# q scaled by its norm over the head's slope where it is made; attention's bias and row maximum by one fused add-scale-minimum per head

## The chip, the core and the metric

The kernel runs on one core of a Trainium2 chip. A core has five engines with one in-order instruction stream each: PE (matmuls; its weight loads are listed as PEld), DVE (the vector engine), ACT (the scalar engine), POOL (GpSimd) and SP, which here only issues DMAs. The metric is device time in microseconds (us), lower is better: the median of three runs was 2928.23 us before the change.

## The reference

A decoder trunk of two layers over 2048 tokens of width 1024: a gated MLP layer, then one layer of dilated sliding-window attention whose keys and values come from a shared projection. Only the attention layer is touched:

```python
q = rms_norm(q, q_norm_g) * (HEAD_DIM ** -0.5)           # per head of 128
# for each of three groups of 8 heads (dilation d = 1, 4, 16), in blocks of 128 queries
sc = jnp.einsum('brnikgh,brnjkh->brnkgij', ql, kb)        # 128 queries x 256 keys (own and previous block)
bias = -slopes * (d * dq)                                 # dq = 128 + i - j
sc = jnp.where(valid, sc + bias, -jnp.inf)
m = jnp.max(sc, axis=-1, keepdims=True)
p = jnp.exp(sc - m)
l = jnp.sum(p, axis=-1, keepdims=True)
o = einsum(p / l, vb);  lse = m + jnp.log(l)
# the groups are then mixed by softmax(lse), gated, and projected out
```

There are 24 query heads, in three groups of 8 with two K/V heads each. Blocks without a previous block see 128 keys, the others 256. `slopes` of head h is 2^(-8(h+1)/24).

## The kernel before

The sequence is cut into four quarters (Q = 0 to 3) of four token tiles of 128. For each quarter the kernel runs the gated MLP layer (`layer_A`: the products v, u, z and o), then the projections of the attention layer (`proj_B`: the K/V blocks `kv_block`, three `q_block`s and a `z_block`). All products are in split precision: each weight tile is loaded by SP (L259, L315), copied to a rounded high part by ACT (L251) and its low part is made by DVE (L252), and PE multiplies three times.

Attention runs as side work ("fillers") between those matmuls. Groups 0 and 1 (`attend_local`) of quarter Q run during `layer_A` of quarter Q+1, and for the last quarter at the very end, between the matmuls of the output projection (`finish`). Group 2 reaches over the whole sequence (`wide_attention`), so it can only start when the last quarter's q of group 2 is stored; it is paced through the last quarter's `kv_block(0)`, `q_block(1)` and `q_block(0)`. One attention unit is a group, a block of 128 queries and one K/V head, with four query heads: 3 x 16 x 2 = 96 units, 42 of them with 128 keys and 54 with 256. Its stages are `att_1` (load of `qt`, transposes `pk` and `pq` on PE, copies to `kT` and `qT`), `att_2` (scores `ps` on PE, bias, maximum, exponentials), `att_3` (transposes `pp` of the probabilities, copy to `pT`), `att_4` (product `po` with the values, copy or sum to `ot`, store).

The code's order isn't the final one: a scheduler with its own cost model sets the order within each engine's stream when the kernel is built, and each stream then runs in that order. The order between engines is kept by semaphores only.

The places that matter here:

- `q_block` (L1215 to L1233). A tile of q of 128 tokens and four heads (512 columns) arrives as `src`. ACT squares it (L1223), DVE sums per head (L1225), and POOL makes four numbers per token with four small instructions (L1226 to L1229): with v the mean square plus epsilon, v^-0.5 goes to columns 516 to 519 of `src` and slope x v^0.5 to columns 512 to 515. q itself stays unscaled. SP stores all 520 columns to `qd` in DRAM (L1232). That store is issued late, five products after; but for group 2 of the last quarter it is only held back by one product (the list `stores` starts at 4 there).
- `att_1` (L1322 to L1351): SP loads `qt` of 520 columns (L1319, two buffers). DVE copies its last 8 columns to `rt` (L1339). PE transposes the four heads (L1343), ACT and DVE make `qT`.
- `att_2` (L1353 to L1404): per head DVE forms `dist` x (slope x v^0.5) + score (L1383, an instruction with one PSUM input; `dist` holds minus the distance, and -1e30 outside the window). It then takes the maximum of the two or four heads that share a PSUM tile (L1386), and makes minus the maximum times v^-0.5 (L1387). For group 0 the result is joined with that of group 1 by a minimum (L1390). ACT takes the exponential per head with v^-0.5 as its scale and L1387's result as its bias (L1393), and sums the row in the same instruction.
- PSUM tiles of attention (`pk`, `pq`, `ps`, `pp`, `po`) share four buffers in the pool `ps`.

Of the kernel before, what the change touches and what calls it, by code (L numbers as in the profile page):

```python
# [12 lines left out]
F32 = mybir.dt.float32  # L13
# [5 lines left out]
P = 128  # L19
D = 1024  # L20
S = 2048
# [13 lines left out]
def trunk(ctx, tc, out, x, c, a_ada_w, a_ada_b, a_norm_g, a_w_in, a_sgu_g, a_w_spatial,  # L35
# [25 lines left out]
    qd = [dp.tile([S, 2, 520], F32, name=f"qd{g}") for g in range(3)]  # L61
# [97 lines left out]
    slopes = cp.tile([P, NH], F32, name="slopes")  # L159
    for h in range(NH):  # L160
        nc.gpsimd.memset(slopes[:, h:h + 1], 2.0 ** (-8.0 * (h + 1) / NH) * DIL[h // 8])
# [380 lines left out]
    def sum_tile(nm):  # L542
        return tp.tile([P, 520], F32, tag="st", name=f"st_{nm}")
# [633 lines left out]
    def proj_B(Q, hk, hb, keep, rest, ahead, ready):  # L1177
# [37 lines left out]
        def q_block(g):  # L1215
            def ev(t, src, n):
                if t < 2 and n == 0:
# [9 lines left out]
                nc.gpsimd.tensor_tensor(src[:, 516:520], s4[:, 4:8], mhalf[:, 0:4], ALU.pow)  # L1227
                nc.gpsimd.tensor_tensor(s4[:, 4:8], s4[:, 4:8], src[:, 516:520], ALU.mult)
                nc.gpsimd.tensor_tensor(src[:, 512:516], s4[:, 4:8],  # L1229
                                        slopes[:, g * 8 + n * 4:g * 8 + n * 4 + 4], ALU.mult)  # L1230
# [86 lines left out]
    def att_q(g, b, kh):  # L1317
        qt = ap_.tile([P, 520], F32, tag="qt", name=f"qt{g}_{b}_{kh}")
        nc.sync.dma_start(qt, blk_rows(qd[g], g, b)[:, kh, :])  # L1319
        return qt  # L1320

    def att_1(u):  # L1322
# [15 lines left out]
        rt = sp.tile([P, 16], F32, tag="rt", name=f"rt{g}_{b}_{kh}")  # L1338
        nc.vector.tensor_copy(rt[:, 0:8], u["qt"][:, 512:520])  # L1339
        u["rt"] = rt  # L1340
# [12 lines left out]
    def att_2(u):  # L1353
# [5 lines left out]
        for c in range(nk):  # L1359
# [21 lines left out]
            for i in range(hp):  # L1381
                h = c * hp + i
                nc.vector.scalar_tensor_tensor(pr[:, i, :], dist[:, 256 - w:256], u["rt"][:, h:h + 1],  # L1383
                                               psc[:, i, :], ALU.mult, ALU.add)
            mx = u["rt"][:, 8 + c * hp:8 + (c + 1) * hp]
            nc.vector.tensor_reduce(mx, pr, AX.X, ALU.max)  # L1386
            nc.vector.scalar_tensor_tensor(mneg, mx, -1.0, u["rt"][:, 4 + c * hp:4 + (c + 1) * hp],  # L1387
                                           ALU.mult, ALU.mult)
            if g == 0:
                nc.vector.tensor_tensor(mneg, mneg, stat[1][:, b, c0:c0 + hp], ALU.min)  # L1390
            for i in range(hp):
                h = 4 + c * hp + i
                nc.scalar.activation(pr[:, i, :], pr[:, i, :], AF.Exp, bias=mneg[:, i:i + 1],  # L1393
                                     scale=u["rt"][:, h:h + 1], accum_out=lsum[:, i:i + 1])
# [318 lines left out]
```

## Time and profile before

| | |
|---|---|
| device time, three runs | 2926.15, 2928.23, 2930.01 us |
| profiled execution, first to last instruction (its span) | 2930.7 us; no other time of that execution is given |
| granted PE clock, mean | 0.998 |
| ACT busy | 1639.0 us, 56% of the span |
| DMA moved | 713.54 MB, mean 243 GB/s |
| `qd` stores and `qt` loads | 96 each of 260 KB; median landing of a `qt` load 3.6 us |

The profile comes from one execution. A group of instructions is named by its line, engine, operation and tiles (output <- inputs), with its count, busy time, mean length in ns, then the engine's idle time just before them and what ended it. In a timeline a row has a start, a length, the engine, the instruction, and in brackets how long its engine had been idle and who ended that. Lengths on an engine overlap: the next instruction often starts before the listed end of the one before, so the distance of two starts is what an instruction really costs its engine. A wait is put down to whatever released it last.

### The profile page before, as it was taken

The page shows a single profiled execution, that of the slowest core. Times are in us where ns is not written, and L with a number is a line of the kernel's source. Part 1 is how long each engine was busy: PE and PEld are TensorE (multiplying, and loading weights), DVE is VectorE, ACT ScalarE, POOL GpSimd, SP SyncE. Part 2 cuts the span into 40 slices and gives each one's busy share as a digit, 9 for nine tenths or more (in the row PEclk, how much of TensorE's full clock was granted, in tenths as well). Part 3 has the DMA queues.
Part 4 walks back from the last instruction along what each step waited for, and adds up shares of the span by engine and source line. Part 5 has one row for each costly group of instructions (what it writes and reads, how often), then busy time and mean ns, then how long its engine had stood idle before and what let it go on. Part 6 is the DMA issues. An engine that isn't in the chain of part 4 may idle for free.

```text
span 2930.7 us, 45684 instructions
## 1 busy us (share of the span) xinstructions
PE 2890.4 (99%) x14642; PEld 2422.7 (83%) x14642; DVE 2166.7 (74%) x4038; ACT 1639.0 (56%) x3378; POOL 758.4 (26%) x1043
## 2 busy tenths in 40 slices
PE   8999999999999999999999999999999999999999
PEld 5788888888888878888888888888888888888887
DVE  6878666787777886877677776877769776888682
ACT  4323355767676365676555365674646366876441
POOL 1057522330000513501223213501414221122312
PEclk9999999999999999999999999999999999999999
DMA  8899976796889976887435976875337967789653
GB/s 285 272 311 336 308 244 184 257 306 203 282 294 315 334 241 210 265 289 249 158 120 202 344 226 203 296 262 162 105 109 260 322 202 224 256 271 332 216 172 112
DMA packets 393813, 713.54 MB, mean 243 GB/s; under 512 B 41723, under 2 KB 141277, under 8 KB 393573
## 3 DMA queue, kind: packets, MB, share of 16 engines
q1 hardware_dynamic: 393572, 710.63, 72.6%
q8 instruction: 116, 1.90, 0.3%
q14 instruction: 125, 1.02, 0.1%
HBM read 552.53 MB, written 157.95 MB: 242 GB/s over the span
## 4 chain that ended last, share of the span: by engine, by line
PE 40%; DMA 3%; issue 3%; DVE 3%; POOL 1%; ACT 1%; SPq 0%; POOLq 0%; ACTq 0%; DVEq 0%
PE po L1453 3%; PE pd_kv L280 3%; PE pd_z L324 2%; PE pd_z L322 2%; PE pd_z L323 2%; PE pd_o3a L280 1%; PE pd_u L322 1%; PE pd_u L324 1%; PE pd_u L323 1%; PE pd_o2a L280 1%; PE pd_v3b L280 1%; PE pf L1637 1%; PE pf L1638 1%; PE pf L1639 1%; DMA qt<-qd 1%
## 5 line engine op out<-in xcount | busy, mean ns | idle before, releaser
L280 PE MATMUL pd_kv<-w_kv,hkh 128*128 128x512 f32 x672 | 209.5, 393 | 1.4 <-DVE w_kv L252 1.3
L322 PE MATMUL pd_u<-hAh,w_u 128*128 128x512 f32 x512 | 207.5, 405 | 0.0
L322 PE MATMUL pd_z<-hAh,w_z 128*128 128x512 f32 x512 | 204.1, 399 | 0.0
L324 PE MATMUL pd_u<-hAh,w_u 128*128 128x512 f32 x512 | 201.0, 393 | 2.3 <-DVE w_u L252 2.3
L323 PE MATMUL pd_u<-hAl,w_u 128*128 128x512 f32 x512 | 200.2, 391 | 0.0
L324 PE MATMUL pd_z<-hAh,w_z 128*128 128x512 f32 x512 | 200.2, 391 | 0.0
L323 PE MATMUL pd_z<-hAl,w_z 128*128 128x512 f32 x512 | 199.5, 390 | 0.0
L1453 PEld LDWEIGHTS po<-kv,pT 128*128 128x128 f32 x1200 | 147.9, 192 | 13.0 <-ACT pT L1299 3.7
L251 ACT ACTIVATE w_u<-raw_u 128x512 fp32r<-128x512 f32 x128 | 79.2, 630 | 135.4 <-DMA raw_u<-in_a_w_in_dram 56.7
L1453 PE MATMUL po<-kv,pT 128*128 128x128 f32 x1200 | 151.2, 276 | 3.6 <-ACT pT L1299 2.5
L251 ACT ACTIVATE w_z<-raw_z 128x512 fp32r<-128x512 f32 x128 | 79.6, 628 | 133.9 <-PE pd_z L324 60.6
L280 PEld LDWEIGHTS pd_kv<-w_kv,hkh 128*128 128x128 f32 x672 | 125.9, 189 | 28.6 <-DVE w_kv L252 2.6
L1401 POOL TENSOR_TENSOR dg<-pr,ident 128x256 f32<-128x256 f32 x38 | 30.9, 813 | 437.2 <-DVE stat L1448 226.6
L252 DVE TENSOR_TENSOR w_z<-raw_z,w_z 128x512 fp32r<-128x512 f32 x128 | 109.4, 868 | 44.9 <-ACT w_z L251 44.6
L280 PE MATMUL pd_kv<-w_kv,hkl 128*128 128x512 f32 x336 | 131.2, 391 | 0.0
L1393 ACT ACTIVATE pr<-pr,stat,rt 128x256 f32<-128x256 f32 (+1 forms) x192 | 104.2, 544 | 33.2 <-DVE stat L1387 20.0
L1226 POOL TENSOR_SCALAR s_q<-s_q 128x4 f32<-128x4 f32 x96 | 26.6, 277 | 351.3 <-DVE s_q L1225 238.8
L252 DVE TENSOR_TENSOR w_u<-raw_u,w_u 128x512 fp32r<-128x512 f32 x128 | 94.1, 745 | 30.8 <-ACT w_u L251 30.0
L324 PEld LDWEIGHTS pd_u<-hAh,w_u 128*128 128x128 f32 x512 | 96.4, 188 | 24.2 <-DVE w_u L252 3.1
L251 ACT ACTIVATE w_q<-raw_q 128x512 fp32r<-128x512 f32 x144 | 88.8, 627 | 48.3 <-PE pd_kv L280 11.2
L252 DVE TENSOR_TENSOR w_q<-raw_q,w_q 128x512 fp32r<-128x512 f32 x144 | 95.8, 687 | 24.9 <-ACT w_q L251 22.9
L324 PEld LDWEIGHTS pd_z<-hAh,w_z 128*128 128x128 f32 x512 | 96.1, 188 | 20.7
(904 smaller groups left out, 8553.1 us busy)
## 6 DMA issues: line engine op xcount, KB each, us to landing
raw_q<-in_b_w_in_dram SPq DMA_DIRECT2D x144, 256.0 KB, 3.4
w_o<-wtd SPq DMA_DIRECT2D x72, 512.0 KB, 5.2
raw_u<-in_a_w_in_dram SPq DMA_DIRECT2D x128, 256.0 KB, 4.2
raw_z<-in_a_w_in_dram SPq DMA_DIRECT2D x128, 256.0 KB, 3.6
wtd<-cs SPq DMA_DIRECT2D x56, 512.0 KB, 4.1
qt<-qd SPq DMA_DIRECT2D x96, 260.0 KB, 3.6
raw_v<-in_a_w_in_dram SPq DMA_DIRECT2D x96, 256.0 KB, 4.1
od<-ot SPq DMA_DIRECT2D x96, 256.0 KB, 3.0
```

Source lines behind the costliest of these rows:

```text
L251: nc.scalar.activation(hi, src, AF.Copy)
L252: nc.vector.tensor_tensor(lo, src, hi.bitcast(F32), ALU.subtract)
L280: last_mm[0] = nc.tensor.matmul(pt, a, u[:, w, :], start=f, stop=e, skip_group_check=more)
L322: nc.tensor.matmul(pts[i], wh, hh[:, k, :], start=k == 0, stop=False)
L323: nc.tensor.matmul(pts[i], wh, hl[:, k, :], start=False, stop=False)
L324: nc.tensor.matmul(pts[i], wl, hh[:, k, :], start=False, stop=k == KT - 1)
L1393: nc.scalar.activation(pr[:, i, :], pr[:, i, :], AF.Exp, bias=mneg[:, i:i + 1], scale=u["rt"][:, h:h + 1], accum_out=lsum[:, i:i + 1])
L1401: nc.gpsimd.tensor_tensor(dg, prev, ident.unsqueeze(1).broadcast_to([P, hp, P]), ALU.mult)
L1453: nc.tensor.matmul(po[:, h * P:(h + 1) * P], u["pT"][h // hp][:, h % hp, j, :], u["kv"][:, j, kh, 1, :], start=j == 0, stop=j == nk - 1)
L1637: nc.tensor.matmul(pt, yb[:, 0, k, :], w_[:, 0, :], start=k == 0, stop=False)
L1638: nc.tensor.matmul(pt, yb[:, 0, k, :], w_[:, 1, :], start=False, stop=False)
L1639: nc.tensor.matmul(pt, yb[:, 1, k, :], w_[:, 0, :], start=False, stop=k == KT - 1)
```

## The change

- q is scaled where it is made: POOL computes v^-0.5, multiplies it by 1 / slope of the head (`steep`), and multiplies all 512 columns of `src` by it, per head, in place. The tiles `src`, `qt` and `qd` lose their 8 extra columns.
- In attention, the copy to `rt`, the bias, the maximum, its scaling and the minimum with group 1 go. In their place stands one `tensor_tensor_reduce` per head: (score + `dist`) x (-slope) is written to `pr`, and its running minimum, which starts from a large number (group 0: from group 1's value), goes to the head's column of `stat`. Because q was divided by the slope, -slope brings minus the biased score.
- ACT's exponential has the constant -1 as its scale.

```diff
-    qd = [dp.tile([S, 2, 520], F32, name=f"qd{g}") for g in range(3)]
+    qd = [dp.tile([S, 2, 512], F32, name=f"qd{g}") for g in range(3)]
...
-    slopes = cp.tile([P, NH], F32, name="slopes")
+    slope = [2.0 ** (-8.0 * (h + 1) / NH) * DIL[h // 8] for h in range(NH)]
+    steep = cp.tile([P, NH], F32, name="steep")
     for h in range(NH):
-        nc.gpsimd.memset(slopes[:, h:h + 1], 2.0 ** (-8.0 * (h + 1) / NH) * DIL[h // 8])
+        nc.gpsimd.memset(steep[:, h:h + 1], 1.0 / slope[h])
...
                 nc.gpsimd.tensor_scalar(s4[:, 4:8], s4[:, 0:4], 1.0 / P, EPS, ALU.mult, ALU.add)
-                nc.gpsimd.tensor_tensor(src[:, 516:520], s4[:, 4:8], mhalf[:, 0:4], ALU.pow)
-                nc.gpsimd.tensor_tensor(s4[:, 4:8], s4[:, 4:8], src[:, 516:520], ALU.mult)
-                nc.gpsimd.tensor_tensor(src[:, 512:516], s4[:, 4:8],
-                                        slopes[:, g * 8 + n * 4:g * 8 + n * 4 + 4], ALU.mult)
+                nc.gpsimd.tensor_tensor(s4[:, 4:8], s4[:, 4:8], mhalf[:, 0:4], ALU.pow)
+                nc.gpsimd.tensor_tensor(s4[:, 4:8], s4[:, 4:8],
+                                        steep[:, g * 8 + n * 4:g * 8 + n * 4 + 4], ALU.mult)
+                heads = src.rearrange("p (h d) -> p h d", d=P)
+                nc.gpsimd.tensor_tensor(heads, heads, s4[:, 4:8].unsqueeze(2).broadcast_to([P, 4, P]),
+                                        ALU.mult)
...
-        rt = sp.tile([P, 16], F32, tag="rt", name=f"rt{g}_{b}_{kh}")
-        nc.vector.tensor_copy(rt[:, 0:8], u["qt"][:, 512:520])
-        u["rt"] = rt
...
             for i in range(hp):
-                h = c * hp + i
-                nc.vector.scalar_tensor_tensor(pr[:, i, :], dist[:, 256 - w:256], u["rt"][:, h:h + 1],
-                                               psc[:, i, :], ALU.mult, ALU.add)
-            mx = u["rt"][:, 8 + c * hp:8 + (c + 1) * hp]
-            nc.vector.tensor_reduce(mx, pr, AX.X, ALU.max)
-            nc.vector.scalar_tensor_tensor(mneg, mx, -1.0, u["rt"][:, 4 + c * hp:4 + (c + 1) * hp],
-                                           ALU.mult, ALU.mult)
-            if g == 0:
-                nc.vector.tensor_tensor(mneg, mneg, stat[1][:, b, c0:c0 + hp], ALU.min)
+                k = g * 8 + c0 + i
+                start = stat[1][:, b, c0 + i:c0 + i + 1] if g == 0 else BIG
+                nc.vector.tensor_tensor_reduce(
+                    out=pr[:, i, :], in0=psc[:, i, :], in1=dist[:, 256 - w:256], scale=-slope[k], scalar=start,
+                    op0=ALU.add, op1=ALU.min, accum_out=mneg[:, i:i + 1])
             for i in range(hp):
-                h = 4 + c * hp + i
                 nc.scalar.activation(pr[:, i, :], pr[:, i, :], AF.Exp, bias=mneg[:, i:i + 1],
-                                     scale=u["rt"][:, h:h + 1], accum_out=lsum[:, i:i + 1])
+                                     scale=-1.0, accum_out=lsum[:, i:i + 1])
```

Built, the fused instruction is two in DVE's stream (both printed as ISA): the one that streams the 128 or 256 columns, and one that writes the accumulated minimum to its column. DVE's stream loses 96 copies, 150 maxima, 150 scalings, 62 minima and 384 bias instructions, and gains 768: 4041 become 3967. Instructions of POOL, PE and SP stay the same in number; ACT's loads of function tables go from 73 to 67.

The scheduler reorders DVE, ACT, POOL and SP around attention; PE's stream is the same, line numbers apart, up to the last units of wide attention (about seven eighths of its instructions), and SP's stream at the start of wide attention keeps its order through the first four `qt` loads.

The first place is DVE at the start of wide attention in the last quarter; `rt_0_0` and `rt_0_1` belong to the units of block 0 and K/V heads 0 and 1, `s_k` is the sum of squares of the K tile and `w_q` a weight's low part. Before:

```order
L1225 TENSOR_REDUCE s_q_1_23746<-hs_q_1_23744 128x4
L1339 COPY rt_0_0_23879<-qt_0_0_23822 128x8
L1339 COPY rt_0_1_23920<-qt_0_1_23872 128x8
L1162 TENSOR_REDUCE s_k_0_23850<-st_hs_k_0_23848 128x4
L1162 TENSOR_REDUCE s_k_1_23858<-st_hs_k_1_23856 128x4
L1165 TENSOR_TENSOR st_hs_k_0_23848<-pd_kv_0_23792,hr_k_0_23852 128x512
L1165 TENSOR_TENSOR st_hs_k_1_23856<-pd_kv_1_23793,hr_k_1_23860 128x512
L252 TENSOR_TENSOR w_q_0_24091<-raw_q_0_24092,w_q_0_24091 128x512
L252 TENSOR_TENSOR w_q_1_24096<-raw_q_1_24097,w_q_1_24096 128x512
L1383 SCALAR_TENSOR_TENSOR pr_0_00_23895<-dist,rt_0_0_23879,ps_0_00_23894 128x128 x4
```

With the change, at the same place:

```order
L1226 TENSOR_REDUCE s_q_1_23432<-hs_q_1_23430 128x4
L1163 TENSOR_REDUCE s_k_0_23536<-st_hs_k_0_23534 128x4
L1163 TENSOR_REDUCE s_k_1_23544<-st_hs_k_1_23542 128x4
L1166 TENSOR_TENSOR st_hs_k_0_23534<-pd_kv_0_23478,hr_k_0_23538 128x512
L1166 TENSOR_TENSOR st_hs_k_1_23542<-pd_kv_1_23479,hr_k_1_23546 128x512
L253 TENSOR_TENSOR w_q_0_23759<-raw_q_0_23760,w_q_0_23759 128x512
L253 TENSOR_TENSOR w_q_1_23764<-raw_q_1_23765,w_q_1_23764 128x512
L1384 ISA pr_0_00_23579,stat_192<-ps_0_00_23578,dist 128x128
L1384 ISA stat_192 128x1
L1384 ISA pr_0_00_23579,stat_192<-ps_0_00_23578,dist 128x128
```

The two copies that needed the loads of `qt` are gone, and nothing else on DVE there reads `qt`; the rest keeps its order.

The second place is POOL just ahead of it, at the last tiles of q of group 2 (`st_q32u`), in the last quarter. Before:

```order
L1226 TENSOR_SCALAR s_q_0_23738<-s_q_0_23738 128x4
L1227 TENSOR_TENSOR st_q32u_23396<-s_q_0_23738,mhalf 128x4
L1228 TENSOR_TENSOR s_q_0_23738<-s_q_0_23738,st_q32u_23396 128x4
L1229 TENSOR_TENSOR st_q32u_23396<-s_q_0_23738,slopes 128x4
L1226 TENSOR_SCALAR s_q_1_23746<-s_q_1_23746 128x4
```

With the change:

```order
L1227 TENSOR_SCALAR s_q_0_23424<-s_q_0_23424 128x4
L1228 TENSOR_TENSOR s_q_0_23424<-s_q_0_23424,mhalf 128x4
L1229 TENSOR_TENSOR s_q_0_23424<-s_q_0_23424,steep 128x4
L1232 TENSOR_TENSOR st_q32u_23082<-st_q32u_23082,s_q_0_23424 128x512
L1227 TENSOR_SCALAR s_q_1_23432<-s_q_1_23432 128x4
```

One of the four instructions of a tile now covers 512 columns in place of 4; the order of the tiles is the same.

The third place is ACT at the first two units of wide attention (`qT` is the copy of the transposed q, `pr` and `b_s` are the score tiles of the two units). Before:

```order
L251 ACTIVATE w_q_1_24096<-raw_q_1_24097 128x512
L251 ACTIVATE w_q_2_24101<-raw_q_2_24102 128x512
L1346 ACTIVATE qT_0_1_23927<-pq_0_1_23922,gqk 128x512
L1393 ACTIVATE pr_0_00_23895,stat_192<-pr_0_00_23895,stat_192,rt_0_0_23879 128x128 x4
L251 ACTIVATE w_q_3_24106<-raw_q_3_24107 128x512
L251 ACTIVATE w_q31t_0_24268<-raw_q31t_0_24269 128x512
L1346 ACTIVATE qT_1_0_23970<-pq_1_0_23965,gqk 128x512
```

With the change:

```order
L252 ACTIVATE w_q_1_23764<-raw_q_1_23765 128x512
L1388 ACTIVATE pr_0_00_23579,stat_192<-pr_0_00_23579,stat_192 128x128 x4
L1346 ACTIVATE qT_0_1_23607<-pq_0_1_23602,gqk 128x512
L252 ACTIVATE w_q_2_23769<-raw_q_2_23770 128x512
L252 ACTIVATE w_q_3_23774<-raw_q_3_23775 128x512
L1388 ACTIVATE b_s,stat_192<-b_s,stat_192 128x128 x4
L1346 ACTIVATE qT_1_0_23646<-pq_1_0_23641,gqk 128x512
```

The exponentials of the first unit now stand ahead of the second unit's `qT`, and two weight copies have moved behind it.

More of the change, by code (lines that the diff above doesn't have):

```diff
@@ L542, in sum_tile @@
     def sum_tile(nm):
-        return tp.tile([P, 520], F32, tag="st", name=f"st_{nm}")
+        return tp.tile([P, 512], F32, tag="st", name=f"st_{nm}")
     def dense_s(ops, b, nm, evac):
@@ L1317, in att_q @@
     def att_q(g, b, kh):
-        qt = ap_.tile([P, 520], F32, tag="qt", name=f"qt{g}_{b}_{kh}")
+        qt = ap_.tile([P, 512], F32, tag="qt", name=f"qt{g}_{b}_{kh}")
         nc.sync.dma_start(qt, blk_rows(qd[g], g, b)[:, kh, :])
```

## The prediction

> **What bounds the kernel now.** I read the page's busy shares first, then the busy time by stretches, then PE's waits.
>
> ```profile
> PE 2890.4 (99%) x14642; PEld 2422.7 (83%) x14642; DVE 2166.7 (74%) x4038; ACT 1639.0 (56%) x3378; POOL 758.4 (26%) x1043
> 952.00:1100.00 148.00, 144.63 (x753) 120.81 (x752) 124.23 (x264) 71.65 (x161) 45.92 (x64) 1.00 0.82 289
> 1611.00:1758.00 147.00, 145.19 (x717) 120.98 (x716) 114.16 (x222) 72.71 (x151) 30.71 (x52) 1.00 0.83 285
> 2271.00:2344.00 73.00, 70.99 (x371) 59.61 (x370) 52.78 (x114) 27.01 (x64) 16.24 (x26) 1.00 0.92 325
> 2420.00:2600.00 180.00, 172.38 (x1142) 153.27 (x1141) 134.59 (x351) 141.15 (x403) 25.58 (x55) 0.99 0.75 240
> 2640.00:2860.00 220.00, 216.16 (x1317) 188.12 (x1316) 172.71 (x432) 117.26 (x326) 56.23 (x33) 1.00 0.70 239
> 2442.00:2448.00 6.00, 5.85 (x31) 5.27 (x32) 4.27 (x11) 4.21 (x13) 0.00 (x0) 0.72 0.57 173
> ```
>
> After the span come PE, PEld, DVE, ACT and POOL busy, the granted clock, DMA. PE is idle for 40 us of 2930.7, so no DVE time counts as such: the change can only give back PE's idle time where attention caused it. In the three stretches that end a quarter's `layer_A` PE idles 3.4 + 1.8 + 2.0 = 7.2 us, under wide attention 180 - 172.4 = 7.6 us, in the last local attention 3.8 us: 18.6 us in all. To these come 6 x (1 - 0.72) = 1.7 us of a halved clock just after PE's longest pauses. About 20 us is the ceiling, 0.7%. Who ended PE's waits from 2400 to 2860:
>
> ```profile
> PE ps L1374 <- ACT qT L1346: 2.6, 2, 1.3
> PE po L1453 <- ACT pT L1299: 2.5, 2, 1.9
> PE pq L1343 <- DVE pr L1383: 2.0, 2, 1.6
> ```
>
> ACT and DVE are late there, though neither is full. The timeline at the start of wide attention says why:
>
> ```profile
> 2407.69 0.19 POOL L1226 TENSOR_SCALAR s_q<-s_q 128x4 f32<-128x4 f32 x1 [8.67 <-DVE s_q L1225]
> 2419.61 0.19 POOL L1226 TENSOR_SCALAR s_q<-s_q 128x4 f32<-128x4 f32 x1 [3.17 <-DVE s_q L1225]
> 2423.17 0.20 POOL L1229 TENSOR_TENSOR st_q32u<-s_q,slopes 128x4 f32<-128x4 f32 x1
> 2427.83 0.32 SPq L1319 DMA_DIRECT2D qt<-qd  x1
> 2430.52 0.17 DVE L1339 COPY rt<-qt 128x8 f32<-128x8 f32 x1 [5.49 <-DMA qt<-qd]
> 2431.05 0.60 PE L1343 MATMUL pq<-ident,qt 128*128 128x128 f32 x4
> 2435.89 1.12 DVE L1383 SCALAR_TENSOR_TENSOR pr<-dist,rt,ps 128x128 f32<-128x128 f32 x4
> 2437.11 0.63 PE L1343 MATMUL pq<-ident,qt 128*128 128x128 f32 x4 [1.59 <-DVE pr L1383]
> 2438.47 0.50 ACT L1393 ACTIVATE pr<-pr,stat,rt 128x128 f32<-128x128 f32 x1 [5.96 <-DVE stat L1387]
> ```
>
> DVE stood 5.5 us at the copy of 8 columns until the second `qt` had landed. Everything behind it (K's norm, weight splits, the first bias) came late; PE waited 1.6 us for a PSUM buffer that this bias reads, ACT 6 us for the maximum, and the exponentials then held up `qT`. The pattern returns later, smaller: DVE waits at the copy, the chain of bias, maximum and scaling is late, ACT's copy behind the exponentials is late, PE waits:
>
> ```profile
> 2502.46 0.17 DVE L1339 COPY rt<-qt 128x8 f32<-128x8 f32 x1 [1.41 <-DMA qt<-qd]
> 2508.11 1.16 PE L1453 MATMUL po<-kv,pT 128*128 128x128 f32 x8 [1.89 <-ACT pT L1299]
> ```
>
> **DVE's part.** Removed, with mean lengths:
>
> ```profile
> L1386 DVE TENSOR_REDUCE rt<-pr 128x2 f32<-128x512 f32 (+1 forms) x75 | 50.9, 679 | 0.2
> L1386 DVE TENSOR_REDUCE rt<-st_pr 128x2 f32<-128x512 f32 (+1 forms) x59 | 40.1, 680 | 0.0
> L1386 DVE TENSOR_REDUCE rt<-b_s 128x4 f32<-128x512 f32 x16 | 10.9, 680 | 0.1
> L1387 DVE SCALAR_TENSOR_TENSOR stat<-rt 128x2 f32<-128x2 f32 (+1 forms) x150 | 25.4, 169 | 0.6
> L1390 DVE TENSOR_TENSOR stat<-stat,stat 128x2 f32<-128x2 f32 (+1 forms) x62 | 12.6, 203 | 0.4
> L1339 DVE COPY rt<-qt 128x8 f32<-128x8 f32 x96 | 21.3, 223 | 77.9 <-DMA qt<-qd 76.5 <-ACT pr L1393 1.1
> L1383 DVE SCALAR_TENSOR_TENSOR b_s<-dist,rt,ps 128x128 f32<-128x128 f32 x64 | 17.9, 342 | 3.7 <-PE ps L1374 3.6
> ```
>
> The maxima are 101.9 us, the rest 25.4 + 12.6 + 21.3 = 59.3: 161 us of listed length, and 76.5 us of waiting for `qt`.
>
> The fused instruction isn't in this trace. It reads the same PSUM tile and `dist` and writes the same tile as L1383, so I take L1383's length (342 ns for 128 columns). Less than that has no reason; twice the streaming is the other end, another 124 ns per 128 columns, since 256 columns take 472:
>
> ```profile
> L1383 DVE SCALAR_TENSOR_TENSOR pr<-dist,rt,ps 128x256 f32<-128x256 f32 x108 | 47.1, 472 | 4.0 <-PE ps L1380 4.0
> 2437.00 0.17 DVE L1339 COPY rt<-qt 128x8 f32<-128x8 f32 x1
> 2437.08 0.68 DVE L1386 TENSOR_REDUCE rt<-pr 128x4 f32<-128x512 f32 x1
> L1393 ACT ACTIVATION_READ_ACCUMULATOR pr<-pr,stat,rt 128x1 f32 x192 | 36.0, 188 | 0.0
> ```
>
> The accumulator write is a one-column instruction. DVE's small copy holds the stream 80 ns from start to start though it is listed with 170; ACT's own accumulator reads are listed with 188. I take 80 ns of stream, between 70 and 188: 384 x 0.08 = 31 us (27 to 72). In stream time the removed maxima are 0.60 each (0.68 less the same overlap of 0.08), 90 us, the small ones 308 x 0.08 = 25 us. Net -84 us of 2167 (with 188 ns: -43; with half the streaming rate too, another 74 us, so +31: 168 heads of 128 columns and 216 of 256 are 600 times 128 columns, x 0.124). The Trainium skill, "VectorE: DVE Perf Modes", section "Two Vector instructions with no wait between them", says that an operation that writes its accumulator is two instructions, as the built stream has it; its formula (N + 151) / 0.96 GHz would make the one-column one an estimated 158 ns and the 384 of them 61 us in place of 31.
>
> What counts is latency per unit. A 128-column unit needs 4 x 0.28 + 0.60 + 0.08 = 1.8 us from the scores to its scale now, when nothing stands between; then ACT can begin. With the change the first column is there after about 0.4 us, the PSUM buffer is free after 4 x (0.28 + 0.08) = 1.4 us (now 1.1), and the wait for `qt` is off DVE. Late next is PE itself at `pq`, which needs the same `qt`.
>
> **POOL's part.** Each of 96 q tiles swaps a 4-column multiplication for one of 512 columns with a repeated scalar, an operation that isn't in the trace. Nearest rows:
>
> ```profile
> L1645 POOL TENSOR_TENSOR of<-of,xr 128x512 f32<-128x512 f32 x32 | 41.5, 1299 | 152.4 <-DVE of L1644 111.3 <-DVE stat L1390 22.0 <-DVE stat L1413 7.4
> L364 POOL TENSOR_TENSOR st_cw<-st_cw,st_cw 128x512 f32<-128x512 f32 x16 | 24.7, 1541 | 1.3
> L1229 POOL TENSOR_TENSOR st_qc<-s_q,slopes 128x4 f32<-128x4 f32 x24 | 8.1, 337 | 1.9
> 1791.69 5.44 PE pd_q21b L280 x24
> ```
>
> I take 1.4 us (1.3 to 1.55, double if the repetition slows it); less 0.3, that is +1.1 per tile, 106 us on an engine busy 26%. Elsewhere the late stores hide it: they are issued five products of 5.44 us (the last row, from the chain of waits: 24 matmuls) after the tile. Not hidden is group 2 of the last quarter. There the last three pairs of tiles come a product or so apart, the first at 2407.7, the last at 2419.6; this last one took POOL 3.8 us, to 2423.4. A pair then takes 3.8 + 2.2 = 6.0 us, more than a product, so lateness piles up: the first pair ends at 2413.7, the second at 2419.7, the last at about 2425.9 instead of 2423.4 with its gaps. The store, then SP's load, land 2.5 us later, 2433.0 instead of 2430.5, and PE, which was at `pq` at 2431.05, stalls **about 2.3 us** (its own order reaches `pq` some 0.3 us after the data now). Queued on SP behind the first stores are the last two K weight loads, about 1.5 us later; the waits above have no row for a K weight, so I cost them at nothing, and at 1.5 us if there were no slack at all. A later `qt` load elsewhere is covered by its second buffer; `qt` rows of 2048 in place of 2080 bytes I cost at nothing beside that.
>
> **ACT.** The same exponentials, six table loads fewer; off PE's path, at nothing.
>
> **The sum**, against the profiled 2930.7: of wide attention's 7.6 + 1.7 = 9.3 us I give back 7, as its waits begin at the copy or the maximum; of the last local attention's 3.8, 1 us (its units share DVE with the output's own sums); of the 7.2 at the ends of `layer_A`, 0.7, as most wait for weights or a norm. Lost: 2.3 for the late `qt`. -7 - 1 - 0.7 + 2.3 = **-6.4 us**, 2924.3 profiled; the profiled span is 2.5 us over the median, so **2921.8** for the median. All waits going gives -20.3 + 2.3 = -18; none going, +2.3.
>
> **Rivals.** (1) *The waits only change place.* Order is fixed by a scheduler, and the copies of ACT and DVE around the units are regrouped; `qT` of the second unit now stands behind the first unit's exponentials, so PE's `ps` can wait there. For it: the waits are 1 to 2 us each and there are under ten, as small as one or two displaced instructions of 0.6 us. Half of the 8.7 us returns: -4.4 + 2.3 = -2 us, 2926. (2) *The fused pair is slow:* at half the streaming rate and 188 ns a unit needs 4 x (0.41 + 0.19) = 2.4 us for its PSUM buffer against 1.1; the removed wait and that delay cancel: 2928. (3) *Slower: POOL's long multiplication collides with DVE.* DVE's weight split, 0.69 us alone, stretches where POOL reads:
>
> ```profile
> L252 DVE TENSOR_TENSOR w_q32t<-raw_q32t,w_q32t 128x512 fp32r<-128x512 f32 x16 | 10.9, 689 | 6.0 <-ACT w_q32t L251 6.0
> 1895.65 1.67 DVE L252 TENSOR_TENSOR w_z2b<-raw_z2b,w_z2b 128x512 fp32r<-128x512 f32 x1
> 1895.17 1.60 POOL L710 TENSOR_TENSOR hAl<-h_a,hAh 128x512 fp32r<-128x512 f32 x1 [4.00 <-ACT hAh L706]
> 219.78:293.04 73.26, 73.26 (x341) 61.23 (x341) 58.89 (x48) 27.58 (x47) 52.66 (x37) 1.00 1.00 336
> ```
>
> One collision costs up to 1.0 us. The Trainium skill, "SBUF — State Buffer", section "Who interferes with whom", has it as a rule: a DVE instruction with two SBUF inputs and a GpSimd instruction that reads SBUF exclude each other, and the later one blocks fully; by this rule, which the trace's pair agrees with, every multiplication added in the q blocks blocks a split or is blocked. At the start of wide attention six multiplications before the last store, each pushed 1 us, add 6 us to the 2.3, while the removed waits still give some 2 back: +6 us, 2934. It decides when a tile's POOL time passes 3.5 us, where a pair falls 1.6 us behind a product. Against it: the last row, an early stretch where POOL is busy 52.7 us of 73.3 and PE never waits.
>
> **How the numbers follow.** Forecast 0.52 (its own range 2914 to 2926), rival 1 0.18, rival 2 0.10, rival 3 0.20. A measurement here can tell about 0.2%, 5.9 us, from no change: faster begins below 2922.4. The forecast is spread about its 2921.8, and as all waits going would give three times as much, two thirds of it is faster, 0.35, with 0.03 of rival 1: 0.38. Slower, over 2934.1, is two thirds of rival 3: 0.13. The rest, 0.49, is within. The range leaves out about a tenth on each side: from 2914, where four fifths of the ceiling return, to 2934, rival 3's time.
>
> **What would show it.** Right: no DVE wait for `qt`; PE's waits on `ps <- qT` and `po <- pT` under 2 us together after 2400; granted clock 1.00 from 2442; PE's wait at the second wide `pq` now for DMA `qt`, 2 to 3 us. The accumulator write spaced 70 to 190 ns; the fused instruction 340 and 470 ns; POOL's multiplication 1.3 to 1.6 us. Wrong: PE idle over 9 us from 2420 to 2600, or new PE waits for weight splits in the q blocks.

## The result, and the profile after

| | before | after |
|---|---|---|
| median of 18 runs each | 2924.95 us (2921.03 to 2930.01) | 2932.19 us (2927.88 to 2937.24) |
| ratio after / before | | 1.0022, 95% interval 1.0015 to 1.0029 |
| span of the profiled execution | 2930.7 us | 2926.2 us |

The changed kernel is slower: by 0.22%, some 6.4 us, by the ratio; the medians lie 7.2 us apart. The forecast was faster, by 6.4 us, to 2921.8. The sign is wrong. The time lies inside the range only because the range was drawn out to rival 3's 2934; the forecast's own ended at 2926. The forecast also started from a median of three runs, 2928.23; taken from the 2924.95 of 18 runs it would have been 2918.6.

The two profiled executions stand the other way round: the one of before is 4.5 us longer. The profiled run of after has the shortest of its 18 times; the span of the one of before is longer than every one of the 18 times of before. At this size one profile of each kernel can't show where the time went; a pause counts only if it comes back in a second profile. Both kernels were therefore profiled again (e1 and e2 below): 2927.1 us before, 2933.4 after.

What was forecast for attention came. The page's busy times after, the busy time by stretches with the columns of the prediction's table, and PE's waits from 2400 to 2860 us:

```profile
PE 2887.2 (99%) x14642; PEld 2419.0 (83%) x14642; DVE 2050.1 (70%) x3964; ACT 1594.3 (54%) x3372; POOL 852.0 (29%) x1043
952.00:1100.00 148.00, 144.82 (x757) 121.05 (x756) 115.80 (x248) 68.00 (x158) 43.14 (x64) 1.00 0.83 293
1611.00:1758.00 147.00, 145.38 (x724) 121.65 (x724) 105.79 (x215) 69.75 (x148) 32.59 (x50) 1.00 0.84 288
2271.00:2344.00 73.00, 71.48 (x376) 60.25 (x375) 48.36 (x113) 24.73 (x58) 16.72 (x26) 1.00 0.92 335
2420.00:2600.00 180.00, 177.58 (x1185) 159.33 (x1184) 115.81 (x396) 134.57 (x411) 44.39 (x67) 1.00 0.79 255
2640.00:2860.00 220.00, 218.17 (x1333) 190.59 (x1333) 136.08 (x402) 113.25 (x336) 58.55 (x33) 1.00 0.69 239
2440.00:2446.00 6.00, 5.35 (x34) 4.68 (x34) 2.84 (x13) 4.74 (x19) 0.00 (x0) 1.00 0.97 305
PE pq L1343 <- DMA qt<-qd: 2.4, 2, 1.8
PE po L1448 <- ACT pT L1302: 0.2, 1, 0.2
```

From 2420 to 2600 us PE is idle 2.4 us in place of 7.6, and all of it is the wait for the late `qt`; the granted clock stays at 1.00 after it; waits on `qT` are gone. What the prediction didn't see lies in the long stretches ahead of that. The same table for three of them, first the second profile of before, then that of after:

```profile
219.78:952.00 732.22, 729.86 (x3447) 607.52 (x3446) 535.87 (x839) 427.18 (x806) 187.43 (x211) 1.00 0.81 273
1100.00:1611.00 511.00, 510.35 (x2565) 431.09 (x2564) 381.00 (x685) 312.00 (x589) 145.18 (x225) 1.00 0.65 213
1758.00:2271.00 513.00, 512.36 (x2585) 430.45 (x2584) 384.71 (x703) 310.28 (x587) 153.57 (x228) 1.00 0.62 200
```

```profile
219.78:952.00 732.22, 728.80 (x3432) 606.35 (x3431) 533.01 (x843) 424.18 (x806) 209.97 (x211) 1.00 0.81 272
1100.00:1611.00 511.00, 507.32 (x2535) 426.69 (x2534) 366.00 (x652) 306.67 (x588) 166.74 (x223) 1.00 0.65 210
1758.00:2271.00 513.00, 509.19 (x2553) 426.17 (x2552) 370.47 (x665) 297.44 (x576) 169.31 (x226) 1.00 0.60 195
```

PE's idle time rises from 2.4 + 0.7 + 0.6 = 3.7 us to 3.4 + 3.7 + 3.8 = 10.9 us. Most of it, 2.8 + 2.8 + 3.0 = 8.6 us, comes at one place in each quarter, where the z block ends and `layer_A` of the next quarter begins. PE's row there, in the first profile of after and in the second:

```profile
639.00 0.70 PE L281 MATMUL pd_v1a<-w_v,hAh 128*128 128x512 f32 x2 [3.19 <-DVE st_z0bw L576]
```

```profile
637.22 0.70 PE L281 MATMUL pd_v1a<-w_v,hAh 128*128 128x512 f32 x2 [2.26 <-DVE st_z0bw L576]
```

Both profiles of before have no wait for that eviction there. The changed kernel's GpSimd time grew by 94 us (758.4 to 852.0), and DVE's weight splits of the z blocks became longer, though nothing in them was changed. Splits of z0 and z2, before and then after:

```profile
L252 DVE TENSOR_TENSOR w_z0bt<-raw_z0bt,w_z0bt 128x512 fp32r<-128x512 f32 x16 | 12.9, 810 | 1.7 <-ACT w_z0bt L251 1.6
L252 DVE TENSOR_TENSOR w_z2bt<-raw_z2bt,w_z2bt 128x512 fp32r<-128x512 f32 x16 | 12.1, 787 | 2.4 <-ACT w_z2bt L251 2.3
```

```profile
L253 DVE TENSOR_TENSOR w_z0bt<-raw_z0bt,w_z0bt 128x512 fp32r<-128x512 f32 x16 | 14.5, 907 | 2.2 <-ACT w_z0bt L252 2.0
L253 DVE TENSOR_TENSOR w_z2bt<-raw_z2bt,w_z2bt 128x512 fp32r<-128x512 f32 x16 | 15.2, 987 | 2.7 <-ACT w_z2bt L252 2.7
```

The row of z2 needs care. In the first profile of after next to none of its 16 splits overlaps a long multiplication; the extra time lies in splits beside L711, GpSimd's subtraction that makes the low part of h (`hAl`), which was there before. L711 now starts as a long multiplication in front of it ends: at 1872.54 and 1891.57, behind multiplications of 1.04 us that began at 1871.54 and 1890.57. So the multiplication can reach a split directly, or by putting L711 off onto it.

That gave three theories: A, GpSimd's long multiplication runs against these splits; B, the scheduler's new order makes the pauses; C, PE merely runs ahead and then stands for loads.

### The profile page after: what moved, and what is told of

Read it like the earlier page. It is cut to its first block, busy times and chain, and to the rows that moved or that the text cites. A ratio compares the mean times of both kernels' runs of the same rounds, so it can differ in the third digit from the quotient of the medians.

```text
span 2926.2 us, 45625 instructions
## 1 busy us (share of the span) xinstructions
PE 2887.2 (99%) x14642; PEld 2419.0 (83%) x14642; DVE 2050.1 (70%) x3964; ACT 1594.3 (54%) x3372; POOL 852.0 (29%) x1043
## 4 chain that ended last, share of the span: by engine, by line
PE 81%; DMA 7%; DVE 4%; issue 3%; ACT 2%; POOL 2%; SPq 1%; POOLq 0%; DVEq 0%; ACTq 0%
PE pd_kv L281 7%; PE po L1448 4%; PE pd_z L323 4%; PE pd_z L325 4%; PE pd_z L324 4%; PE pd_u L323 4%; PE pd_u L325 4%; PE pd_u L324 4%; PE pm L1042 2%; PE pd_o L281 2%; PE pd_o2a L281 1%; PE pd_o3a L281 1%; PE pq L1343 1%; PE ps L1374 1%; PE pd_o1a L281 1%
## 5 line engine op out<-in xcount | busy, mean ns | idle before, releaser
L1423 POOL TENSOR_TENSOR pT<-pT,dg 128x256 f32<-128x256 f32 x76 | 58.6, 771 | 231.7 <-DVE pT L1422 197.6
L1388 ACT ACTIVATE pr<-pr,stat 128x256 f32<-128x256 f32 (+1 forms) x192 | 86.3, 452 | 67.0 <-DVE stat L1384 66.8
L1227 POOL TENSOR_SCALAR s_q<-s_q 128x4 f32<-128x4 f32 x96 | 33.5, 349 | 299.7 <-DVE s_q L1226 294.2
```

Source lines behind the costliest of these rows:

```text
L1227: nc.gpsimd.tensor_scalar(s4[:, 4:8], s4[:, 0:4], 1.0 / P, EPS, ALU.mult, ALU.add)
L1423: nc.gpsimd.tensor_tensor(pT[:, :, 0, :], pT[:, :, 0, :], u["dg"][:, c * hp:(c + 1) * hp, :], ALU.add)
```

## The experiments

All ratios are to the kernel before, timed on the same chip beside each group of runs. "Long" is the multiplication of 512 columns on GpSimd, "short" one of 4 columns in its place, which leaves q unscaled.

| run | multiplication | bias and maximum | median, us | ratio, 95% interval |
|---|---|---|---|---|
| e1_before | none | old | 2927.75 | 1.0004 (0.9994 to 1.0014) |
| e2_after | long | fused | 2932.64 | 1.0024 (1.0015 to 1.0032) |
| e3_small_mult | short | fused | 2913.87 | 0.9960 (0.9947 to 0.9972) |
| e4_old_bias | long | old, no copy | 2933.70 | 1.0026 (1.0015 to 1.0037) |
| e5_pow | a power of 4 columns | fused | 2919.58 | 0.9988 (0.9979 to 0.9997) |
| e6_g0_small | short for group 0 | fused | 2915.41 | 0.9968 (0.9955 to 0.9980) |
| e7_act_mult | on ScalarE | fused | 2997.30 | 1.0250 (1.0236 to 1.0265) |
| e8_dve_mult | on VectorE | fused | 3067.41 | 1.0489 (1.0475 to 1.0503) |
| e9_mixed | none for group 0, else long | old for group 0, else fused | 2919.31 | 0.9980 (0.9969 to 0.9990) |
| e10_old_bias_small | short | old, no copy | 2919.50 | 0.9982 (0.9973 to 0.9990) |
| e11_g12_small | long for group 0 only | fused | 2926.51 | 1.0003 (0.9993 to 1.0014) |
| e12_swap | as e6, blocks swapped | fused | 2929.55 | 1.0013 (1.0004 to 1.0022) |

**e1 and e2: both kernels again.** No edit.

> The kernel before, unchanged, for a second profile and for the granted clock of its runs. If the difference between the two kernels is in the pauses of PE that the two first profiles show, PE waits here again from 2420 to 2600 us (7 us or more idle), and not at the end of the z blocks near 635, 1275 and 1915 us (under 2 us idle in all three together). Pauses that appear in one profile and not in the other are chance and explain nothing. Ratio 0.999 to 1.001.

> The changed kernel, unchanged, for a second profile. If the loss lies at the end of the z blocks, PE waits there again: 2 to 4 us near 635, 1 us or more near 1275 and near 1915. If those waits were chance, they are gone here while the time stays at a ratio of 1.0022.

The pauses of both first profiles came back, as the rows above show. So they belong to the kernels. That PE paused again near 1275 and 1915 us is in the two last rows of the table by stretches. In e1 PE stands 2.4 us in all at the three places, for other things, a little more than the 2 us that I allowed.

**e3: the multiplication made short.** The order on PE, DVE and ACT stays exactly that of the change; on SP one instruction moves.

```diff
-                heads = src.rearrange("p (h d) -> p h d", d=P)
-                nc.gpsimd.tensor_tensor(heads, heads, s4[:, 4:8].unsqueeze(2).broadcast_to([P, 4, P]),
-                                        ALU.mult)
+                nc.gpsimd.tensor_tensor(src[:, 0:4], src[:, 0:4], s4[:, 4:8], ALU.mult)
```

> The changed kernel with the multiplication of 512 columns on GpSimd cut to 4 columns, so q goes unscaled and the scores are wrong; the order on PE, DVE and ACT stays as it is. Theory A (the long multiplication runs against DVE's weight splits in the K/V, q and z blocks, loads are taken up late and PE pauses): the loss goes and the gain in wide attention stays, 2916 to 2921 us, ratio 0.996 to 0.999, and the mean of the w_z2bt split falls from 987 back to about 790 ns. Theory B (the scheduler's other order of DVE, ACT and SP makes the loss): the time stays at 2930 to 2934, ratio 1.002. Theory C (PE runs ahead and then waits for weight loads that DMA brings no faster): it stays too, or falls by under 2 us.

It went even below theory A's range. Against e2 it gains 1.0024 - 0.9960 = 0.0064, some 18.7 us, and against the kernel before it is faster by 0.40%, 11.7 us. B and C fall: with the same order, and with PE further ahead than in the change, PE doesn't wait. As the order is the same, each PE instruction of e2 can be set beside its twin in e3. PE's lag grows by 4.2, 3.0, 3.0 and 4.6 us across the ends of the four z blocks, 14.8 of the 21.2 us by which e2's profile is longer, and by 2.0 us at the late `qt`. The end of the first q block and the z block, in e2 and then in e3:

```profile
562.00:592.00 30.00, 30.00 (x138) 24.84 (x137) 26.74 (x40) 20.02 (x35) 17.78 (x25) 1.00 0.89 294
592.00:637.00 45.00, 42.96 (x201) 35.16 (x199) 36.56 (x55) 23.97 (x43) 24.27 (x25) 1.00 0.87 287
```

```profile
562.00:592.00 30.00, 30.00 (x138) 24.83 (x137) 25.43 (x41) 20.10 (x35) 13.69 (x25) 1.00 0.91 298
592.00:637.00 45.00, 45.00 (x211) 37.20 (x210) 35.16 (x57) 26.51 (x46) 16.76 (x21) 1.00 0.90 298
```

Third to fifth number of a row are PE's loads, DVE and ACT; the last ones the clock, the DMA share and GB/s. DVE is busy 85 to 89% of the first stretch and DMA about 90% of both, in either kernel: there is little room in which lost time could be made up. In e2 DVE does 40 + 55 instructions in 63.3 us; in e3 it does 41 + 57, three more, in 60.6. Eight splits of e2 between 560 and 637 us overlap a long multiplication by half a microsecond or more and take 10.26 us together; undisturbed they would take 8 x 0.68 = 5.44, so DVE loses 4.8 us. That is about its lag: DVE is 0.6 us behind e3 near 545 us and 5.0 at the eviction that PE will wait for (`st_z0bw`, at 636.39 and 631.38), while PE is 0.9 behind until it must wait (its last z product at 629.36 and 628.43) and 5.1 after it. SP then issues the first load for the next product (`raw_v`) at 626.89 us with the long multiplication and at 621.45 with the short one, and PE takes that product up at 637.22, after its wait, and at 633.87, with none:

```profile
626.89 1.36 SPq L260 DMA_DIRECT2D raw_v<-in_a_w_in_dram  x2
```

```profile
621.45 1.52 SPq L260 DMA_DIRECT2D raw_v<-in_a_w_in_dram  x2
633.87 0.62 PE L281 MATMUL pd_v1a<-w_v,hAh 128*128 128x512 f32 x2
```

ACT starts on that load at 633.62 in e2, 6.7 us after its issue, and at 628.60 in e3, 7.2 us after. The load is no slower in e2; it is issued later. Just before the pause in e2 the other engines hardly work, and the pause is followed by a lower clock:

```profile
630.00:634.50 4.50, 4.50 (x21) 3.72 (x21) 0.22 (x1) 0.85 (x2) 0.00 (x0) 1.00 1.03 396
634.50:637.20 2.70, 0.46 (x3) 0.04 (x2) 2.70 (x6) 1.66 (x4) 0.58 (x1) 1.00 0.71 272
637.20:640.50 3.30, 3.28 (x10) 2.69 (x11) 2.95 (x5) 2.73 (x5) 0.71 (x1) 0.69 0.88 277
640.50:643.50 3.00, 3.00 (x11) 2.34 (x10) 1.49 (x3) 1.23 (x2) 0.00 (x0) 0.77 0.81 227
```

DVE works 0.22 of 4.5 us while DMA is full at 396 GB/s; then all comes at once, DVE is full for 2.7 us and PE waits for an eviction that stands behind the splits. The chain as I read it: a split is late, so its `raw` buffer comes free late, so SP issues the next load late, into a DMA that is nearly full in either kernel. The first link and the last are tested by e3 and e5; the buffer between them is read from the trace only, as no run changes the number of `raw` buffers. From 560 to 640 us SP stood for the splits of `w_z0bt`, in e2 and then in e3:

```profile
SPq L260 <- DVE w_z0bt L253: 8.0, 8, 2.3
```

```profile
SPq L260 <- DVE w_z0bt L253: 4.9, 7, 1.5
```

Part of the lag takes another way: just ahead of the late `raw_v`, SP stands 4.1 us in e2 and 2.6 in e3 for the stored h (`m<-hd`), which DVE makes too.

**e5: the same GpSimd time without the memory traffic.**

```diff
+                nc.gpsimd.tensor_tensor(src[:, 0:4], s4[:, 4:8], mhalf[:, 0:4], ALU.pow)
```

in place of e3's short multiplication.

> The changed kernel with the long multiplication on GpSimd replaced by a power of 4 columns, an instruction that holds GpSimd nearly as long (1.0 to 1.3 us in the profiles so far) but reads and writes almost nothing; q stays unscaled, so the scores are wrong. The order on PE, DVE and ACT is that of the changed kernel. Theory A1 (the multiplication's reads of SBUF hold up DVE's splits): 2913 to 2918 us, as with the short multiplication (2913.9). Theory A2 (GpSimd is late, and with it the stores of q and the low parts of h for which SP and PE stand): 2928 to 2934, as with the long one (2932.6). In between, both count, each by its share of 18.8 us.

It landed between: 0.0036 of the 0.0064 is gone without the traffic, some 10.5 us; 0.0028, some 8 us, is there with GpSimd's time alone. One multiplication beside one split, in the changed kernel, and the power at the same place:

```profile
597.83 1.04 POOL L1232 TENSOR_TENSOR st_q00w<-st_q00w,s_q 128x512 f32<-128x512 f32 x1
598.21 1.21 DVE L253 TENSOR_TENSOR w_z0bt<-raw_z0bt,w_z0bt 128x512 fp32r<-128x512 f32 x1
```

```profile
596.11 1.01 POOL L1231 TENSOR_TENSOR st_q00w<-s_q,mhalf 128x4 f32<-128x4 f32 x1
596.93 0.68 DVE L253 TENSOR_TENSOR w_z0bt<-raw_z0bt,w_z0bt 128x512 fp32r<-128x512 f32 x1
560.00:640.00 80.00, 80.00 (x369) 66.17 (x368) 64.24 (x105) 52.06 (x89) 43.60 (x51) 1.00 0.92 308
```

The split that starts under the multiplication takes 0.53 us longer, a little less than the 0.66 us that the multiplication still runs; the one under the power takes its 0.68. And in the stretch of the first z block PE doesn't wait at all. What is left of the cost is elsewhere: in the same profile PE waits 3.3 us for the late `qt` of wide attention and 2.0 us in the last z block.

```profile
PE pq L1343 <- DMA qt<-qd: 3.3, 2, 2.6
PE pd_z3bb L281 <- ACT w_z3b L252: 2.0, 1, 2.0
```

That profile has the shortest of e5's 11 times, so these two don't account for all 8 us of the medians. And the splits are not left alone everywhere: those of z2 take longer than the 727 ns of e3, and all of the extra time lies in the seven that overlap L711, as GpSimd's time puts L711 off here too. PE doesn't pause for it: from 1758 to 2271 us it idles 1.2 us, as in e3. A longer split by itself is not yet a pause.

```profile
L253 DVE TENSOR_TENSOR w_z2bt<-raw_z2bt,w_z2bt 128x512 fp32r<-128x512 f32 x16 | 14.2, 916 | 3.8 <-ACT w_z2bt L252 3.8
```

**e6, e11 and e12: which of the 96 multiplications.** In e6 those of group 0 are short, in e11 those of groups 1 and 2; the order of PE, DVE and ACT is that of the change in both. In e12 the kernel e6 has its q blocks in another order, so that group 1, with long multiplications, stands ahead of the z block:

```diff
-        q_block(1)
         q_block(0)
+        q_block(1)
```

> The changed kernel with the short multiplication for group 0 only (32 of 96 tiles, those that are evicted in the last q block and into the z block); the scores of group 0 are wrong. The order on all engines is kept. If the loss comes from the tiles beside the z block's weight splits, more than half of the 18.8 us goes: 2918 to 2923 us, and the pauses near 635, 1275 and 1915 us fall below 1 us each. If each multiplication costs the same wherever it is, a third goes: about 2926.

> The changed kernel with the long multiplication for group 0 only and the short one for groups 1 and 2 (their scores are wrong): the complement of the kernel that shortened group 0. If the costs add up, the 32 multiplications of group 0 cost here what their removal gave, 16 us over 2913.9: 2928 to 2932 us, ratio 1.001 to 1.003. If it takes all three groups to fill the engines, it is 2918 to 2924.

> The kernel with the short multiplication for group 0 (2915.4 us), with the q blocks of groups 0 and 1 in swapped order, so that group 1, whose tiles have the long multiplication, now stands last, right ahead of the z block (the scores of group 0 are wrong). If the place beside the z block makes the cost, PE pauses again at the end of the z blocks and the time rises by about 12 us, the cost of 32 long multiplications there: 2924 to 2931 us, ratio 1.000 to 1.003. If it is something of group 0 itself, it stays at 2914 to 2919, ratio 0.996 to 0.998.

Taking group 0's 32 multiplications away gives 1.0024 - 0.9968 = 0.0056, 16 us, beyond the 2918 that I expected at best; having them alone costs 1.0003 - 0.9960 = 0.0043, 13 us, a little below the range that I gave. The other 64 alone cost 0.9968 - 0.9960 = 0.0008, which the intervals can't tell from nothing. In e6's profile PE idles 1.8 + 0.1 + 1.5 = 3.4 us in the three long stretches, as in the kernel before, and of the eight long splits near the first z block two are left. e12 points to the place and not the group: with group 1 last it is 1.0013, 0.0045 above e6, and the z splits are long again (e6, then e12):

```profile
L253 DVE TENSOR_TENSOR w_z2bt<-raw_z2bt,w_z2bt 128x512 fp32r<-128x512 f32 x16 | 11.3, 728 | 4.9 <-ACT w_z2bt L252 4.9
```

```profile
L253 DVE TENSOR_TENSOR w_z2bt<-raw_z2bt,w_z2bt 128x512 fp32r<-128x512 f32 x16 | 15.1, 978 | 3.1 <-ACT w_z2bt L252 3.1
PE pd_z3bb L281 <- ACT w_z3b L252: 3.4, 1, 3.4
```

PE idles 3.2, 0.4 and 4.1 us in the three long stretches of e12 and waits 3.4 us in the last z block, so the pauses are back in three quarters of four. The other order of the blocks moves more than the multiplications, and no run has it with all of them short; what the swap costs by itself stays open.

**e4 and e10: the fused instruction apart from the copy.** Both have q scaled where it is made and no copy to `rt`, but the old bias and maximum; e10 has the short multiplication.

```diff
+                nc.vector.scalar_tensor_tensor(pr[:, i, :], dist[:, 256 - w:256], 1.0, psc[:, i, :],
+                                               ALU.mult, ALU.add)
+            nc.vector.tensor_reduce(mx, pr, AX.X, ALU.max)
+            nc.vector.tensor_tensor(mneg, mx, minus[:, k:k + hp], ALU.mult)
...
-                                     scale=-1.0, accum_out=lsum[:, i:i + 1])
+                                     scale=slope[k + i], accum_out=lsum[:, i:i + 1])
```

> q is scaled on GpSimd as in the change and no copy waits for qt, but the bias, the maximum and its scaling are made by the old kind of instructions in place of the fused one. Theory A: the loss of the multiplication is all here, 2930 to 2936 us, ratio 1.002 to 1.004. Theory B: the order is a third one, so it may land anywhere from 2922 to 2934. If the fused instruction were what costs (rival 2 of the prediction), this kernel would be faster than the changed one by 5 us or more.

> The kernel with the old bias and maximum and no copy to rt (2933.7 us), with the short multiplication on GpSimd, so q goes unscaled and the scores are wrong; the order on PE, DVE and ACT is that of the kernel with the old bias. If the gain comes from the copy that waited for qt, and the fused instruction as such adds little, this lands with the fused kernel with the short multiplication (2913.9): 2913 to 2918 us, ratio 0.996 to 0.998. If the shorter chain of the fused instruction is what gains, it stays at 2920 or above.

e4 pays the whole loss, as theory A said. e10 is a miss by 1.5 us at the range's upper end: without the multiplication the missing copy alone gives 0.0018, 5 us, and the fused instruction another 0.0022, 6 us (the two intervals just don't touch). With the long multiplication in place the fused instruction gains nothing that the intervals show (e2 1.0024, e4 1.0026), so the 6 us are no fixed price. In wide attention the copy was all that mattered. From 2420 to 2600 us in e10:

```profile
2420.00:2600.00 180.00, 180.00 (x1198) 161.88 (x1197) 138.46 (x338) 140.11 (x419) 31.09 (x62) 1.00 0.80 257
```

PE has no idle time left there, with the old instructions on DVE (138.5 us of 180, as before). So what the fused one adds lies elsewhere. In e10's profile, the longest of its 11 times, PE idles 3.2 us from 219.78 to 952, 2.3 from 1100 to 1611 and 4.3 from 2640 to 2860, against 1.0, 0.5 and 2.2 in e3; I didn't separate what causes it.

**e7 and e8: the multiplication on another engine.**

```diff
-                nc.gpsimd.tensor_tensor(heads, heads, s4[:, 4:8].unsqueeze(2).broadcast_to([P, 4, P]),
+                nc.vector.tensor_tensor(heads, heads, s4[:, 4:8].unsqueeze(2).broadcast_to([P, 4, P]),
```

for e8; e7 has four `nc.scalar.activation` per tile with the factor as scale.

> The changed kernel with q scaled on ScalarE, by four instructions of 128 columns per tile, in place of GpSimd. The computation is whole. ScalarE gets 384 instructions of about 0.3 us more, 115 us on an engine with 1594 us. Theory A1: nothing collides with DVE's splits any more: 2915 to 2922 us, ratio 0.996 to 0.999, faster than both kernels. Against it: ScalarE's copies of the weights then stand behind the scaling, which waits for the norm, so PE's pauses could stay: 2926 or more.

> The changed kernel with q scaled on VectorE by one multiplication of 512 columns per tile. The computation is whole. VectorE gets 96 instructions of about 0.69 us, 0.60 in its stream, 58 us. Theory A1 prices a collision at 0.4 to 0.9 us of VectorE per tile, so this is about as dear as what it replaces: 2922 to 2932 us, between the changed kernel and the one on ScalarE. Theory A2 has GpSimd free again: 2914 to 2920.

Both are clear misses: e7 is 71 us above the 2926 that I named as the case against it, e8 135 us above its range. I had priced the instructions, not the wait in front of them. What ACT (e7) and DVE (e8) waited for at this line, us and times:

```profile
  POOL s_q L1229: 80.4, 84
```

```profile
  POOL s_q L1229: 125.9, 96
```

The factor comes from GpSimd; each multiplication stands in the stream until it is there (1.3 us each on DVE), and the weight copies and splits behind it stand too. The orders of DVE, ACT and SP are others in both runs, so this is read from the traces and not separated from the order.

**e9: group 0 as before, groups 1 and 2 as in the change.** In the code, `if g == 0:` selects the old lines in `q_block`, `att_1` and `att_2`.

> Group 0 as in the kernel before (q unscaled, 520 columns, copy to rt, old bias, maximum and minimum), groups 1 and 2 as in the change. The computation is whole. If the 32 long multiplications of group 0 carry nearly all of the loss (2915.4 us without them, 2932.6 with them) and the gain is in wide attention, which is group 2, this beats both kernels: 2914 to 2919 us, ratio 0.996 to 0.998. If group 0's copies and maxima took part of the gain with them, it ends at 2920 to 2924.

2919.31 us, a ratio of 0.9980 (0.9969 to 0.9990): faster than both kernels, by 0.2% and 0.4%, with the whole computation. It misses 2919 by 0.3 us and doesn't reach e6, which is what group 0's copies and old maxima cost, or the order, which is another one. In its profile the first z block has no pause, and wide attention keeps its gain:

```profile
592.00:637.00 45.00, 45.00 (x213) 37.19 (x212) 36.03 (x58) 27.21 (x47) 18.97 (x24) 1.00 0.91 306
2420.00:2600.00 180.00, 178.32 (x1189) 160.08 (x1188) 119.01 (x407) 139.30 (x425) 40.01 (x64) 1.00 0.81 260
```

## Why the prediction was wrong

- **What bounds the kernel, the 20 us ceiling: right.** e3, which keeps the order and leaves the long multiplication out, gained 11.7 us of it, and e10 left no idle time in wide attention.
- **DVE at the copy is why PE waits in wide attention: right.** The 7 us that I gave back there were too few. With no late `qt` all comes back: PE idle 180 - 179.5 = 0.5 us in e3 in place of 7.6, and no lower clock.
- **The prices of the instructions: near.** In the profile of after:

```profile
L1384 DVE CUSTOM_DVE_ANT_0 pr<-ps,dist 128x128 f32<-128x128 f32 x80 | 18.4, 286 | 2.3 <-PE ps L1374 2.2
L1384 DVE CUSTOM_DVE_ANT_0 pr<-ps,dist,stat 128x256 f32<-128x256 f32 x60 | 25.6, 478 | 10.3 <-PE ps L1380 10.1
L1384 DVE DVE_READ_ACCUMULATOR2_ANT stat<- 128x1 f32 x384 | 31.6, 82 | 0.0
L1232 POOL TENSOR_TENSOR st_qc<-st_qc,s_q 128x512 f32<-128x512 f32 x24 | 29.9, 1245 | 1.9
```

  I took 342 and 472 ns for the fused instruction, 80 for the accumulator write, 1.4 us for the multiplication. "Less than that has no reason" was wrong: it is 286 ns. What I left out is that L1383 reads its factor from a column of SBUF and the fused instruction has constants: the old instruction with a constant factor, in e10, takes 281 ns.

```profile
L1387 DVE SCALAR_TENSOR_TENSOR pr<-dist,ps 128x128 f32<-128x128 f32 x84 | 18.5, 281 | 17.8 <-PE ps L1378 17.8
```

  The accumulator write takes 82 ns, near my 80 and not the 158 set beside it. Rival 2 (half the streaming rate, 188 ns) falls; its 124 ns per 128 columns should have been 472 - 342 = 130, and nothing hangs on that.
- **The late `qt`, 2.3 us: right.** PE waits 2.4 and 2.3 us there in the two profiles of after.
- **"Elsewhere the late stores hide it": this step failed.** I asked only who waits for the multiplication's result, and the answer, nobody, was nearly right: from 596 to 632 us SP stands 1.6 us for GpSimd at the late stores in e2, against 0.4 in e1, and e5, where it stands 1.9 us there, has no pause in that block. I didn't ask what the multiplication takes from its neighbours. Its price outside wide attention was 0; by e6 the 32 multiplications ahead of the z blocks cost 16 us. -8.7 from attention, +2.3 for `qt` and +16 would have been +9.6; +6.4 was measured. The sign of being wrong that I named, new waits for splits in the q blocks, was near it: in e2 those are 0.7 and 0.6 us, for weight copies, and the pauses stand one block later.
- **Rival 3 had the mechanism, and the wrong place.** It let the collision act at the start of wide attention, through the store of q, and priced it by GpSimd's own delay. There it did little. I set it aside because of an early stretch in which GpSimd is busy 52.7 of 73.3 us and PE never waits. But that row says (x48) for DVE in 73 us; the z block's row in e2 has 55 in 45 us. My reading is that a collision is hidden where DVE has few instructions to do per microsecond and costs where it has many; no run tests that by itself, and DMA is full in the early row as well (1.00). The Trainium skill's page "SBUF — State Buffer", section "Who interferes with whom", gives the rule that I cited for the rival, that the later of the two instructions blocks fully; the split above, 0.53 us longer under a multiplication with 0.66 us to run, nearly agrees with it, and the power, which reads four columns, left the split beside it as it was.
- **The last local attention and the ends of `layer_A`, 1 and 0.7 us:** PE's idle time there is 1.8 us for 3.8, and 6.3 for 7.2, in the first profile of after. The first is not steady: the last z block's pause falls into the same stretch in the second profile.

## What to carry to other kernels

Off the critical path is not free: before moving work to an idle engine, look at what else runs in the stretch where it lands, and ask both who waits for its result and which neighbour it slows. The stretch to ask about is the one like the last q block and z block here, where DVE is busy for 81 to 89% (e2), DMA for about 90%, and PE still doesn't wait: 4.8 us lost on DVE there came back as 4.2 us on PE. And when a sum of effects is 0.2%, take more than one profile of each kernel before believing a place, and hold the order of the engines fixed when one cost is taken out.

## What the runs showed of the hardware

- What a DVE instruction costs here depends on whether its scalar is a constant or a column of SBUF, and hardly on which of the two instructions it is. `scalar_tensor_tensor` takes 342 and 472 ns for 128 and 256 columns with its factor in a column, 281 and 410 with a constant (e10). The fused add, scale and minimum takes 286 and 417 ns with a constant start value, and 478 for 256 columns with its start value in a column.
- A pause of PE of 2.3 us was followed by a lower clock: 0.69 over the next 3.3 us and 0.77 over the 3.0 after them (the rows from 637.20 in e2), another 0.31 x 3.3 + 0.23 x 3.0 = 1.7 us. One of 1.78 us, up to 1916.62 in the same profile, was not (1.00 from 1917 to 1920). The Trainium skill's page "TensorE: Matmul & The Clock Gate", section "HAM oscillation — how this bites in real kernels", names gaps over about 3.4 us; here a shorter one did it.
- A GpSimd multiplication of 512 columns by a repeated scalar takes 1.04 us when nothing is in its way, less than the 1.30 us of the multiplication of two full tiles that was my nearest row.
